# The mixers' residual gate, moved from the output weights to the output products

## Chip, core and metric

The kernel runs on one core of a Trainium2 chip. The metric is the device time of one execution in microseconds (us). Engines are named as the profile names them: PE is TensorE's matmuls, PEld its weight loads, DVE is VectorE, ACT is ScalarE, POOL is GpSimd, SP is SyncE, which issues most of the DMAs. L835 is line 835 of the kernel before.

## What is computed

Two layers of a streaming encoder over 256 tokens of width 1024, in float32. The place of the change is the first residual of each layer: a vector `1 + g_m`, one number for each of the 1024 columns, scales the output projection of three token mixers.

```python
def reference(x, c, positions, w_ada, ...):
    for l in range(DEPTH):                       # 2
        mod = (c_act @ w_ada[l] + b_ada[l])[:, None, :]
        sh_m, sc_m, g_m, sh_f, sc_f, g_f = jnp.split(mod, 6, axis=-1)
        h = x * (1.0 + sc_m) + sh_m
        mix = token_mixers(h, w_in[l], w_out[l], ...)     # [attention | retention | mLSTM] @ w_out
        x = layer_norm(DEEPNORM_ALPHA * x + (1.0 + g_m) * mix, ln_mix_g[l], ln_mix_b[l])
        h = x * (1.0 + sc_f) + sh_f
        y = moe_ffn(h.reshape(bsz * seq, d), w_router, b_router, w_gate[l], w_up[l], w_down[l])
        x = layer_norm(DEEPNORM_ALPHA * x + (1.0 + g_f) * y.reshape(bsz, seq, d), ...)
    return x
```

Since the gate scales columns, `(1 + g_m) * (o @ W)` is the same as `o @ (W * (1 + g_m))`.

## The kernel before

**Tiles.** Tokens lie on the 128 partitions in two tiles (tt = 0, 1), columns in halves of 512 (n = 0, 1). A product in float32 is split into a rounded part and a rest (`wsplit`: L415 casts the high part on ACT, L416 subtracts it on DVE), and three matmuls (L434 to L436) make one product of the two.

**Weights.** All weights come over one stream of DMAs on SP's queue, in an order written out by hand (`st.add` lines), into pools of buffers. A DMA is issued when its buffer is free, and everything behind it in the queue waits for it. The pool `ring` has 10 buffers of 512 KB, `w` 8, and `g0` one: it holds the mixers' gate `g1[l][0]`, and after it a down projection weight of the experts, ("dn", l, 1, 2).

**Order.** Each engine works through its instructions in a fixed order. A scheduler sets it when the program is built, with a simulated time line and priorities (`tc.high_priority`, `tc.issue_after`). So an edit at one place can change the order at others.

**The stage of the output projection**, once in each layer:

1. Retention and attention still finish: scores of retention on PE (L716), masked on DVE (L791, L792), sums over them on PE (L739), a norm on ACT and DVE with a matmul between (L760, L811, L812), attention's sums (L827), and the split of the mixers' output (L768, L769). Small instructions of the adaptive norm stand in between on DVE (L406, L411, L841 to L843, L935).
2. `out_w` fetches a tile of w_out (two blocks of 128 x 512); POOL multiplies each block in place with the gate (L917), with a high priority. `wsplit` splits it. Then PE multiplies (`out_part`): 16 blocks, each for two token tiles, three matmuls each. The four sums (tt, n) stay in four banks of PSUM; the last blocks close tile 0's two halves first, then tile 1's.
3. PE goes on with half of the sums of the adaptive norm (`ada_half`, L349, L353).
4. For each token tile, DVE forms the residual of two halves from x and PSUM (`residual`, L835), takes statistics of it (`lstat`, L442, L444), ACT makes the inverse deviation (rs, L210), and DVE normalizes 1024 columns (L957). PE transposes (L850), ACT and DVE copy (L961), PE multiplies with the router's weights (L963). ACT and POOL split the normalized tile (L972, L973). After tile 1 the router chooses experts, and the experts' stage (the MoE) begins.

POOL's memset of the next residual's buffer (`xrow`, L1039) waits for the last reading of x in step 4, since both use the same buffer. In the experts' stage PE multiplies (L1208, L1256, L1281), and DVE adds gathered rows (L1162).

Of the kernel before, what the change touches and what calls it, by code (L numbers as in the profile page):

```python
# [16 lines left out]
OP = mybir.AluOpType  # L17
# [10 lines left out]
ALPHA = (2.0 * L) ** 0.25  # L28
# [7 lines left out]
AHEAD_SPLIT = 400  # L36
# [78 lines left out]
def _trunk(ctx, tc, x_tok, x_chn, par, pos, rows, b_ada, w_ada, w_idx, w_in, w_out, w_gu, w_dn, out):  # L115
    nc = tc.nc
    V, A, G, PE = nc.vector, nc.scalar, nc.gpsimd, nc.tensor
# [17 lines left out]
    st = Stream(tc, sb, AHEAD)  # L135
# [10 lines left out]
    for l in range(L):  # L146
# [24 lines left out]
        st.add(("gu2", l, 1), w_gu[l, 1], 4, "S", range(2))  # L171
        st.add(("gu", l, 1), w_gu[l, 1], 8, which=(4, 5, 6, 7))
        st.add(("dn", l, 1), w_dn[l, 1], 4, "P", (0, 1))
        st.add(("dn", l, 1), w_dn[l, 1], 4, "g0", (2,))
        st.add(("gu4", l, 0), w_gu[l, 0], 16, "w", range(12, 16))
        st.add(("dn4", l, 1), w_dn[l, 1], 8, "w", (6, 7))
        st.add(("gu4", l, 2), w_gu[l, 2], 16, "w", (14, 15))
        st.add(("gu2", l, 2), w_gu[l, 2], 4, "O", (0,))
        st.add(("gu", l, 2), w_gu[l, 2], 8, which=range(2, 7))
# [649 lines left out]
            out_split(2 * g, 2, po)  # L829
        return oT  # L830

    def residual(z, x, p, tt, n):

        o = slice(tt * D + n * 512, tt * D + n * 512 + 512)
        V.scalar_tensor_tensor(z[:, o], x[:, o], ALPHA, p[tt][n], op0=OP.mult, op1=OP.add)  # L835
        return z[:, o]

    def make_aff(gcol, bcol, sc, sh, name):
# [15 lines left out]
    for l in range(L):  # L854
# [55 lines left out]
        def out_w(n, j):  # L910

            if j % 2 == 0:
                out_w.w = st.get(("out", l, n, j // 2))
                for i in range(2):
                    q = out_w.w[:, i * 512:(i + 1) * 512]
                    with tc.high_priority(offset=AHEAD_SPLIT):
                        G.tensor_tensor(q, q, g1[l][0][:, n * 512:(n + 1) * 512], op=OP.mult)  # L917
            return wsplit(out_w.w[:, (j % 2) * 512:(j % 2) * 512 + 512])

        for ns, js in (((0,), (0, 1, 2, 3)), ((1,), (0, 1, 2, 3)), ((0, 1), (4, 5))):  # L920
# [31 lines left out]
            for (la, na), q in zip(LAST[l], pa):  # L952
                ada_half(q, la, na, 0, True)
        for tt in range(2):
            m, rs = lstat([residual(z, xres, pd, tt, n) for n in range(2)])
            o = slice(tt * D, (tt + 1) * D)
            V.tensor_scalar(xn[:, o], z[:, o], m[:, 0:1], rs, op0=OP.subtract, op1=OP.mult)  # L957
            for k0 in (0, 4):
                pt = transposed(xn, tt, k0)
                q = h2[:, tt * D + k0 * P:tt * D + (k0 + 4) * P]  # L960
                (A.copy if k0 == 0 else V.tensor_copy)(q, pt)  # L961
                for k in range(k0, k0 + 4):
                    last = PE.matmul(pl[:, tt * E:(tt + 1) * E], h2v[:, tt, k, :], wrg[:, k, :], start=False, stop=(tt == 1 and k == KD - 1))  # L963
# [408 lines left out]
```

## Time and profile before

| | |
|---|---|
| runs | 730.05 us median of 3 (729.27 to 730.53) |
| profiled execution | 729.74 us |
| its span in the profile | 728.0 us |
| PE busy | 667.6 us (92%), mean granted clock 0.957 |
| DVE busy | 414.1 us (57%) |
| ACT busy | 280.9 us (39%) |
| POOL busy | 208.2 us (29%) |
| DMA | 204.19 MB, mean 280 GB/s |

The page's shares are means over stages with different limits. What one stage costs is read from its time line: which engine works without a pause, and what ends the pauses of the others. The granted clock is 1.00 where TensorE runs at 2.4 GHz and 0.50 where it runs at 1.2 GHz.

### The profile page before, as it was taken

The page shows a single profiled execution, that of the slowest core. Times are in us where ns is not written, and L with a number is a line of the kernel's source. Part 1 is how long each engine was busy: PE and PEld are TensorE (multiplying, and loading weights), DVE is VectorE, ACT ScalarE, POOL GpSimd, SP SyncE. Part 2 cuts the span into 40 slices and gives each one's busy share as a digit, 9 for nine tenths or more (in the row PEclk, how much of TensorE's full clock was granted, in tenths as well). Part 3 has the DMA queues.
Part 4 walks back from the last instruction along what each step waited for, and adds up shares of the span by engine and source line. Part 5 has one row for each costly group of instructions (what it writes and reads, how often), then busy time and mean ns, then how long its engine had stood idle before and what let it go on. Part 6 is the DMA issues. An engine that isn't in the chain of part 4 may idle for free. (4 is left out here: it accounts for less than half of the span.)

```text
span 728.0 us, 10437 instructions
## 1 busy us (share of the span) xinstructions
PE 667.6 (92%) x3638; PEld 409.9 (56%) x3638; DVE 414.1 (57%) x903; ACT 280.9 (39%) x583; POOL 208.2 (29%) x195
## 2 busy tenths in 40 slices
PE   5999699999898999999888999999899799999994
PEld 0567587864675434434347678885568554433431
DVE  5478986653975321243477999754645632234245
ACT  3346758344332212122256646944523212222131
POOL 3002933101913046102035613310740303712001
PEclk9999989999897999999998999999969789999998
DMA  8997773499986899999945773439958578999951
GB/s 305 407 368 241 258 267 112 144 363 409 377 299 236 310 322 349 370 408 407 365 156 172 235 256 116 144 125 319 396 183 276 187 264 304 354 353 407 406 193 58
DMA packets 57760, 204.19 MB, mean 280 GB/s; under 512 B 7336, under 2 KB 7464, under 8 KB 56422
## 3 DMA queue, kind: packets, MB, share of 16 engines
q1 hardware_dynamic: 55152, 198.49, 75.5%
q0 software_dynamic: 2112, 4.44, 1.6%
q8 instruction: 30, 0.49, 0.3%
q10 hardware_dynamic: 438, 0.54, 0.2%
q14 instruction: 28, 0.23, 0.1%
HBM read 202.15 MB, written 4.19 MB: 283 GB/s over the span
## 5 line engine op out<-in xcount | busy, mean ns | idle before, releaser
L416 DVE TENSOR_TENSOR sb_w<-sb_ring,sb_w 128x512 fp32r<-128x512 f32 (+1 forms) x156 | 117.1, 764 | 42.6 <-ACT sb_w L415 40.6
L415 ACT CAST sb_w<-sb_ring 128x512 fp32r<-128x512 f32 (+1 forms) x156 | 92.1, 608 | 89.0 <-PE ps_mm L435 44.2
L1208 PE MATMUL ps_s<-sb_ring,sb_S 128*64 128x512 f32 x424 | 116.2, 600 | 0.2 <-PEq L1117 0.2
L435 PE MATMUL ps_mm<-sb_w,sb_H 128*128 128x512 f32 (+2 forms) x224 | 79.9, 359 | 4.3 <-DVE sb_H L888 4.3
L434 PE MATMUL ps_mm<-sb_w,sb_H 128*128 128x512 f32 (+2 forms) x224 | 80.2, 365 | 1.9 <-ACT sb_w L415 1.3
L436 PE MATMUL ps_mm<-sb_w,sb_H 128*128 128x512 f32 (+2 forms) x224 | 74.9, 369 | 0.7 <-DVE sb_w L416 0.6
L917 POOL TENSOR_TENSOR sb_ring<-sb_ring,sb_g 128x512 f32<-128x512 f32 x32 | 45.5, 1460 | 72.0 <-DMA sb_ring<-w_out 70.8
L1208 PEld LDWEIGHTS ps_s<-sb_ring,sb_S 128*64 128x64 f32 x424 | 32.5, 136 | 54.0 <-issue 45.9
L349 PE MATMUL ps_t<-sb_ring,cact 128*32 128x512 f32 x272 | 47.7, 616 | 7.8 <-DVE posf L296 6.2
L434 PEld LDWEIGHTS ps_mm<-sb_w,sb_H 128*128 128x128 f32 x224 | 43.0, 194 | 10.7 <-ACT sb_w L415 2.8
L435 PEld LDWEIGHTS ps_mm<-sb_w,sb_H 128*128 128x128 f32 x224 | 43.3, 194 | 10.1 <-DVE sb_H L888 5.0
L436 PEld LDWEIGHTS ps_mm<-sb_w,sb_H 128*128 128x128 f32 x224 | 41.7, 194 | 11.6 <-issue 3.8
L1107 DVE TENSOR_SCALAR sb_S<-ps_t,afffg,afffb 128x256 f32<-128x256 f32 x32 | 17.4, 543 | 48.9 <-ACT sb_S L210 48.4
L1099 PEld LDWEIGHTS ps_t<-sb_O,sb_H 128*128 128x128 f32 x256 | 33.1, 193 | 19.9 <-issue 11.4
L1256 PE MATMUL ps_t<-sb_P,sb_sg 128*64 128x512 f32 x152 | 42.4, 599 | 0.5 <-ACT sb_sg L1243 0.5
L528 POOL TENSOR_TENSOR sb_rope<-sb_rope 128x256 f32<-128x256 f32 (+1 forms) x16 | 15.8, 990 | 89.3 <-DVE iwm L564 31.5
L435 PE MATMUL ps_mm<-sb_H,sb_w 128*128 128x256 f32 x128 | 37.3, 292 | 3.9 <-DVE sb_w L416 3.9
L1099 PE MATMUL ps_t<-sb_O,sb_H 128*128 128x256 f32 x256 | 39.0, 297 | 2.0 <-DVE sb_O L1029 1.8
L633 POOL TENSOR_SCALAR sb_sg<-sb_sg,sm 128x128 f32<-128x128 f32 (+1 forms) x32 | 26.6, 847 | 45.5 <-DVE sm L630 23.3
L210 ACT ACTIVATE sb_S<-ps_t,afffb,afffg 128x256 f32<-128x256 f32 x32 | 18.0, 563 | 55.9 <-PE ps_t L1099 55.1
L434 PE MATMUL ps_mm<-sb_H,sb_w 128*128 128x256 f32 x128 | 37.1, 291 | 0.0
L436 PE MATMUL ps_mm<-sb_H,sb_w 128*128 128x256 f32 x128 | 36.9, 288 | 0.0
(369 smaller groups left out, 1234.1 us busy)
## 6 DMA issues: line engine op xcount, KB each, us to landing
sb_ring<-w_gu SPq DMA_DIRECT2D x106, 512.0 KB, 7.4
sb_ring<-w_ada SPq DMA_DIRECT2D x96, 512.0 KB, 6.9
sb_P<-w_dn SPq DMA_DIRECT2D x58, 512.0 KB, 7.9
sb_ring<-w_in SPq DMA_DIRECT2D x56, 512.0 KB, 6.1
sb_ring<-w_out SPq DMA_DIRECT2D x16, 512.0 KB, 10.1
sb_S<-w_gu SPq DMA_DIRECT2D x6, 1024.0 KB, 8.4
sb_row<-rows SPq DMA_DIRECT2D x8, 512.0 KB, 9.6
sb_w<-w_gu SPq DMA_DIRECT2D x12, 256.0 KB, 4.7
```

Of the source, the lines that this page charges most:

```text
L210: return A.activation(o, i, f, bias=bias, scale=scale)
L349: PE.matmul(pa[32 * g:32 * g + 32, :], cact[:, k:k + 1].to_broadcast([P, 32]), w[g // 2][:, (g % 2) * 512:(g % 2) * 512 + 512], start=(i = ...
L415: A.copy(hi, src)
L416: V.tensor_tensor(lo, src, hi.bitcast(F32), op=OP.subtract)
L434: PE.matmul(o, a[0], b[0], start=start, stop=False)
L435: PE.matmul(o, a[1], b[0], start=False, stop=False)
L436: return PE.matmul(o, a[0], b[1], start=False, stop=stop)
L633: G.tensor_scalar(sg[:, i * n:(i + 1) * n], sg[:, i * n:(i + 1) * n], sm[:, h:h + 1], None, op0=OP.mult)
L917: G.tensor_tensor(q, q, g1[l][0][:, n * 512:(n + 1) * 512], op=OP.mult)
L1099: last = PE.matmul(pt[:, j * 256:(j + 1) * 256], src[:, tt * D + k * P:tt * D + (k + 1) * P], oh[:, tt * D + q * 256:tt * D + (q + 1) * 25 ...
L1208: PE.matmul(pgu[s * 64:s * 64 + 64, :], xg[:, c0:c0 + 64], ws[s][k], start=(i == order[0] and k == 0), stop=(i == order[3] and k == 1), ti ...
L1256: PE.matmul(pyb[s * 64:s * 64 + 64, :], hdT[:, k, s * 64:s * 64 + 64], wd[s][k], start=(k == 0), stop=(k == 1), tile_position=(0, 64 * s))
```

## The change

The gate no longer multiplies the weights. `out_w` loses the two POOL products for each tile of w_out. `residual` gets the gate and becomes two DVE instructions: the product of PSUM with the gate into z, then `ALPHA * x + z` in place. The gate is now read until the residual, so its buffer comes free later, and the weight that takes it over, ("dn", l, 1, 2), stands two entries later in the stream.

```diff
         st.add(("dn", l, 1), w_dn[l, 1], 4, "P", (0, 1))
-        st.add(("dn", l, 1), w_dn[l, 1], 4, "g0", (2,))
         st.add(("gu4", l, 0), w_gu[l, 0], 16, "w", range(12, 16))
         st.add(("dn4", l, 1), w_dn[l, 1], 8, "w", (6, 7))
+        st.add(("dn", l, 1), w_dn[l, 1], 4, "g0", (2,))
...
-    def residual(z, x, p, tt, n):
+    def residual(z, x, p, g, tt, n):
 
         o = slice(tt * D + n * 512, tt * D + n * 512 + 512)
-        V.scalar_tensor_tensor(z[:, o], x[:, o], ALPHA, p[tt][n], op0=OP.mult, op1=OP.add)
+        V.tensor_tensor(z[:, o], p[tt][n], g[:, n * 512:(n + 1) * 512], op=OP.mult)
+        V.scalar_tensor_tensor(z[:, o], x[:, o], ALPHA, z[:, o], op0=OP.mult, op1=OP.add)
         return z[:, o]
...
                 out_w.w = st.get(("out", l, n, j // 2))
-                for i in range(2):
-                    q = out_w.w[:, i * 512:(i + 1) * 512]
-                    with tc.high_priority(offset=AHEAD_SPLIT):
-                        G.tensor_tensor(q, q, g1[l][0][:, n * 512:(n + 1) * 512], op=OP.mult)
...
-            m, rs = lstat([residual(z, xres, pd, tt, n) for n in range(2)])
+            m, rs = lstat([residual(z, xres, pd, g1[l][0], tt, n) for n in range(2)])
```

The scheduler then orders the engines anew. Three places, all in layer 0; lines of the changed kernel are one higher from the residual on (its product is L835, its second instruction L836), and three lower behind `out_w` (L957 is L954 there, L961 is L958, L963 is L960).

DVE at the residual, before (sb_H is z, bs and mv are the statistics):

```order
L835 SCALAR_TENSOR_TENSOR sb_H<-sb_X,ps_mm 128x512
L442 BN_STATS bs<-sb_H 128x6
L835 SCALAR_TENSOR_TENSOR sb_H<-sb_X,ps_mm 128x512
L442 BN_STATS bs<-sb_H 128x6
L835 SCALAR_TENSOR_TENSOR sb_H<-sb_X,ps_mm 128x512
L444 BN_AGGR mv<-bs 128x2
L442 BN_STATS bs<-sb_H 128x6
L835 SCALAR_TENSOR_TENSOR sb_H<-sb_X,ps_mm 128x512
L957 TENSOR_SCALAR sb_H<-sb_H,mv,rs 128x1024
L442 BN_STATS bs<-sb_H 128x6
L444 BN_AGGR mv<-bs 128x2
L957 TENSOR_SCALAR sb_H<-sb_H,mv,rs 128x1024
```

The same place after, behind the first product (sb_g_631 is the gate):

```order
L836 SCALAR_TENSOR_TENSOR sb_H<-sb_X,sb_H 128x512
L835 TENSOR_TENSOR sb_H<-ps_mm,sb_g_631 128x512
L442 BN_STATS bs<-sb_H 128x6
L836 SCALAR_TENSOR_TENSOR sb_H<-sb_X,sb_H 128x512
L835 TENSOR_TENSOR sb_H<-ps_mm,sb_g_631 128x512
L442 BN_STATS bs<-sb_H 128x6
L835 TENSOR_TENSOR sb_H<-ps_mm,sb_g_631 128x512
L836 SCALAR_TENSOR_TENSOR sb_H<-sb_X,sb_H 128x512
L444 BN_AGGR mv<-bs 128x2
L836 SCALAR_TENSOR_TENSOR sb_H<-sb_X,sb_H 128x512
L442 BN_STATS bs<-sb_H 128x6 x2
L954 TENSOR_SCALAR sb_H<-sb_H,mv,rs 128x1024
```

All four products stand ahead of the first normalization, and so does the last statistic, which came behind it before; layer 1 has the same order.

ACT at the end of retention, before (sb_e<-ps_s is the square of L739's sums):

```order
L820 COPY sb_S<-ps_mm 128x512 x2
L415 CAST sb_w<-sb_ring 128x512
L210 ACTIVATE sb_e<-ps_s 128x512
L415 CAST sb_w<-sb_ring 128x512 x2
L210 ACTIVATE sb_e<-ps_s,epsc 128x512
```

The same place after:

```order
L820 COPY sb_S<-ps_mm 128x512 x2
L415 CAST sb_w<-sb_ring 128x512 x3
L210 ACTIVATE sb_e<-ps_s 128x512
L415 CAST sb_w<-sb_ring 128x512 x3
L210 ACTIVATE sb_e<-ps_s,epsc 128x512
```

Two more blocks of w_out are cast ahead of the square, for which ACT waits on PE.

PE at the router, before (L850 transposes, L963 is the router's product):

```order
L850 MATMUL ps_t<-ident,sb_H 128x128 x8
L963 MATMUL ps_s<-wrg,sb_O 128x16 x4
L850 MATMUL ps_t<-ident,sb_H 128x128 x4
L963 MATMUL ps_s<-wrg,sb_O 128x16 x4
L850 MATMUL ps_t<-ident,sb_H 128x128 x4
L963 MATMUL ps_s<-wrg,sb_O 128x16 x8
```

The same place after:

```order
L851 MATMUL ps_t<-ident,sb_H 128x128 x8
L960 MATMUL ps_s<-wrg,sb_O 128x16 x8
L851 MATMUL ps_t<-ident,sb_H 128x128 x8
L960 MATMUL ps_s<-wrg,sb_O 128x16 x8
L349 MATMUL ps_mm<-sb_ring,cact 32x512 x8
```

Four of tile 0's router products move from behind tile 1's first transposes to ahead of them, which is the order that layer 1 had already.

## Rows read from the trace of the kernel before

**Rows 1.** The page's part 5: busy, mean of one, idle ahead, and its releaser.

```profile
L917 POOL TENSOR_TENSOR sb_ring<-sb_ring,sb_g 128x512 f32<-128x512 f32 x32 | 45.5, 1460 | 72.0 <-DMA sb_ring<-w_out 70.8
```

**Rows 2.** Time line of POOL in layer 0: start, length, instruction, idle ahead.

```profile
179.47 24.30 POOL L917 TENSOR_TENSOR sb_ring<-sb_ring,sb_g 128x512 f32<-128x512 f32 x16 [39.13 <-DMA sb_ring<-w_out]
218.45 1.80 POOL L1039 MEMSET sb_X<- 128x2048 f32 x1 [14.68 <-DVE sb_H L835]
221.96 2.34 POOL L973 TENSOR_TENSOR sb_H<-sb_H 128x1024 fp32r<-128x1024 f32 x1 [1.71 <-ACT sb_H L972]
```

**Rows 3.** Time line of PE in layer 0.

```profile
181.87 1.45 PE L716 MATMUL ps_s<-sb_S 64*128 64x256 f32 x8 [1.24 <-DVE sb_S L792]
185.46 2.83 PE L739 MATMUL ps_s<-sb_S 128*64 128x128 f32 x24 [2.15 <-DVE sb_S L792]
...
225.88 1.72 PE L963 MATMUL ps_s<-wrg,sb_O 128*128 128x16 f32 x8
```

**Rows 4.** Time line of DVE in layer 0, end of retention.

```profile
177.36 0.16 DVE L411 TENSOR_TENSOR modc<-mod,bada 128x4 f32<-128x4 f32 x1
...
179.47 1.81 DVE L769 TENSOR_TENSOR sb_O<-sb_e,sb_O 128x512 fp32r<-128x512 f32 x1 [0.68 <-ACT sb_O L768]
...
182.46 1.19 DVE L411 TENSOR_TENSOR modc<-mod,bada 128x4 f32<-128x4 f32 x1
183.69 1.19 DVE L841 TENSOR_TENSOR affmg<-pr,modc 128x8 f32<-128x8 f32 x1
...
185.33 0.77 DVE L842 TENSOR_TENSOR affmb<-pr,modc 128x8 f32<-128x8 f32 x1
...
186.36 0.28 DVE L792 TENSOR_TENSOR sb_S<-ps_s,dec 128x128 f32<-128x128 f32 x1
```

**Rows 5.** Time line of DVE in layer 0, residual and normalization.

```profile
213.60 0.69 DVE L835 SCALAR_TENSOR_TENSOR sb_H<-sb_X,ps_mm 128x512 f32<-128x512 f32 x1 [0.67 <-PE ps_mm L436]
...
217.70 0.69 DVE L835 SCALAR_TENSOR_TENSOR sb_H<-sb_X,ps_mm 128x512 f32<-128x512 f32 x1
218.30 2.50 DVE L957 TENSOR_SCALAR sb_H<-sb_H,mv,rs 128x1024 f32<-128x1024 f32 x1
...
222.34 2.51 DVE L957 TENSOR_SCALAR sb_H<-sb_H,mv,rs 128x1024 f32<-128x1024 f32 x1 [0.70 <-ACT rs L210]
```

**Rows 6.** Time line of DVE in layer 1, end of retention.

```profile
522.12 1.31 DVE L416 TENSOR_TENSOR sb_w<-sb_ring,sb_w 128x512 fp32r<-128x512 f32 x1 [1.59 <-ACT sb_w L415]
...
523.55 1.02 DVE L411 TENSOR_TENSOR modc<-mod,bada 128x4 f32<-128x4 f32 x1
...
525.80 0.68 DVE L772 TENSOR_TENSOR sb_e<-ps_s,sb_e 128x512 f32<-128x512 f32 x1
...
547.19 0.68 DVE L769 TENSOR_TENSOR sb_O<-sb_e,sb_O 128x512 fp32r<-128x512 f32 x1
```

**Rows 7.** Time line of PE in layer 1.

```profile
526.53 1.65 PE L716 MATMUL ps_s<-sb_S 64*128 64x256 f32 x4 [2.88 <-DVE sb_e L772]
...
568.91 1.09 PE L850 MATMUL ps_t<-ident,sb_H 128*128 128x128 f32 x8 [1.36 <-DVE sb_H L957]
...
573.06 1.94 PE L850 MATMUL ps_t<-ident,sb_H 128*128 128x128 f32 x8 [0.63 <-DVE sb_H L957]
```

**Rows 8.** Stretches: length, busy of PE, PEld, DVE, ACT, POOL, clock, DMA, GB/s.

```profile
183.80:190.60 6.80, 5.14 (x29) 4.25 (x30) 6.38 (x9) 1.62 (x3) 6.80 (x6) 0.50 1.04 417
190.60:217.60 27.00, 27.00 (x160) 21.42 (x158) 22.72 (x27) 10.94 (x20) 13.17 (x8) 1.00 0.91 315
...
525.40:538.60 13.20, 11.36 (x32) 7.98 (x34) 7.45 (x16) 1.85 (x3) 10.71 (x9) 0.50 0.52 193
```

**Rows 9.** The same view of a stretch of layer 0's experts.

```profile
310.00:330.00 20.00, 19.44 (x81) 7.95 (x78) 8.96 (x16) 4.62 (x9) 1.81 (x1) 1.00 1.03 409
```

**Rows 10.** Waits of PE, and of PEld, from 236 to 364: total, times, longest.

```profile
PE ps_t L1241 <- DVE sb_rope L1239: 1.8, 1, 1.8
...
PEld ps_s L1208 <- DMA sb_P<-w_dn: 0.3, 1, 0.3
```

## The prediction

> **What bounds the kernel now.** I read the page first: TensorE is busy most of the time, so what counts is where PE pauses, and where it runs at the lower of its two clocks. Then I read the time lines of POOL, PE and DVE side by side in the two stages that the change touches, the end of retention with the output projection and the residual with the router, and last the waits of PE in the experts' stage.
>
> In layer 0 POOL multiplies weights without a break from 179.47 to 203.77 [rows 2]; both layers together cost it 45.5 us [rows 1]. POOL itself is waited for by few. But DVE instructions that read two inputs from SBUF are slow in just that time. L411 on 4 columns takes 0.16 us with POOL idle and 1.19 with POOL at work; L769 takes 1.81, and 0.68 in layer 1 after POOL's last product [rows 4, 6]. Those slow instructions stand ahead of L791 and L792 in DVE's order, and PE waits on L792 twice, for 1.24 and 2.15 us [rows 3]. After that PE has no pause to the end of the output projection [rows 8]. So in this stage the path to the end runs through DVE up to about 186.6 (the last L792 ends there [rows 4]), and through PE from there. Layer 1 has the same picture: L416 takes 1.31, L411 1.02, and PE waits 2.88 us on L772 [rows 6, 7]. In both places TensorE's granted clock then is 0.50, that is 1.2 GHz, for 6.8 and 13.2 us, with 5.14 and 11.36 us of PE work in it [rows 8].
>
> In the tail the path runs through DVE again: residual, statistics, normalization L957, and PE's transposes wait for L957 (1.36 and 0.63 us in layer 1 [rows 7]). L957 itself takes 2.5 us, and why is seen from POOL: the memset runs from 218.45 to 220.25 and L957 ends at 220.80; L973 runs from 221.96 to 224.30 and the second L957 ends at 224.85 [rows 2, 5]. Both times L957 ends 0.55 us after POOL.
>
> **The change part by part.** The sum is made against the profiled execution, 729.74 us (a span of 728.0 and 1.74 around it). The median of the runs is 0.31 above that.
>
> *The holes, layer 0.* Without POOL's products, L769 falls from 1.81 to 0.69 and L411 from 1.19 to 0.16, and L841, as small as L411, from 1.19 to the same 0.16 [rows 4, 6]. That is 1.12 + 1.03 + 1.03 = 3.2 us ahead of the L792 that starts L739. L842 gives 0.6 more (0.77 to 0.16) ahead of the last L792, which lets L739 finish: 3.8. Behind it PE is dense, so this moves the whole rest of the stage. I take 3.5, between the two ends. The new order has nothing that gives it back: ACT casts two blocks more ahead of the square, but ACT waited there anyway, and the DMA of the blocks was ahead of POOL, whose products ran without a pause [rows 2].
>
> *The holes, layer 1.* L416 falls from 1.31 to 0.69 and L411 from 1.02 to 0.16. From L411's end at 524.57 to L772 at 525.80 there are 1.23 us with L841 and L842 [rows 6]. In the new order L935 and L843 go ahead of L772 as well: three small ones at 0.16 and one of 128 columns at about 0.28 (L792's time [rows 4]) are 0.76. So 0.62 + 0.86 + 0.47 = 1.9 us. The ends are 1.5 (what the gaps between instructions may keep) and 3.0 (if PE's four L716, 1.65 us at the lower clock [rows 7], still run at the higher one). I take 1.9.
>
> *The clock.* If TensorE keeps 2.4 GHz through the shorter holes, half of its work there is saved: 5.14 / 2 = 2.6 us in layer 0, 11.36 / 2 = 5.7 in layer 1 [rows 8]; if it falls as before, nothing. In layer 0 the 3.4 us of pauses shrink to a few tenths, so I take 2.0 of the 2.6. In layer 1 nearly a microsecond of waiting on L772 is left, and thin work around it, so I take nothing. Ends: 0 and 8.3.
>
> *The tail's DVE.* Four products are added in each layer. From the first L835 at 213.60 to the last at 217.70 six instructions (and L444) pass, 0.68 us each [rows 5]. In the new order nine stand ahead of the last L836, since all four products come first: 3 x 0.68 = 2.05 us later. A product from PSUM is priced as L835 was, 0.69, since that read PSUM and SBUF too; the second instruction, now all from SBUF, as L769 with POOL idle, 0.68. POOL's memset follows the last reading of x, and L957 ends 0.55 behind the memset, so L957 moves by 2.05 and no more: the two statistics that now stand ahead of it run beside the memset. ACT's cast and POOL's L973 follow L957, and the second L957 follows L973: 2.05 again.
>
> What PE makes of it differs. In layer 1 PE waits for both L957 already, so all of it is paid: 2.05 at least, 3.0 if the clock falls sooner and the first eight transposes take 1.94 instead of 1.09 [rows 7]. I take 2.1. In layer 0 router products of tile 0, 1.72 us [rows 3], stood behind tile 1's transposes. They now fill the longer wait: between 2.05 - 1.72 = 0.3 and 2.05. I take 1.2. In all DVE gets 8 x 0.69 = 5.5 us more, of which 3.3 is on the path.
>
> The Trainium skill, SBUF — State Buffer, section on the two separate sides, says that DVE and GpSimd take turns on one pair of ports, with an exclusive lock: the one that comes second waits for the whole instruction of the other. The two endings 0.55 behind POOL agree [rows 2, 5]. If the pair were shared by bandwidth instead, L957 would keep its 2.5 us and start 2.05 + 2 x 0.68 later, 3.4 in each layer, and the sum below would be 2.7 us worse. The rule also speaks against the change: L836 reads two inputs from SBUF, which L835 did not, and so could be blocked; but POOL idles for 14.68 us up to the memset [rows 2].
>
> *The queue.* The DMA into the gate's buffer now waits for the last product, and behind it stand only weights of later experts. Cost nothing; the tiles around it wait for PE's last blocks anyway. If that cover were gone, it would hold the queue for 2 us, the tail's delay.
>
> *The experts' order.* The scheduler moves some L1162, L1208 and L1281. PE's longest pause there is 1.8 us, on a DVE instruction [rows 10]; I take 0, with 1.8 either way.
>
> Sum: -3.5 - 1.9 - 2.0 + 1.2 + 2.1 + 0 = -4.1. The profiled execution goes to 725.6, the median to 726.0, with a range of its own from 722.0 to 729.0.
>
> **Rivals.**
>
> *The clock stays high in both holes.* Then 8.3 instead of 2.0 is saved: 719.7. For it: the holes lose most of their idle time. Against: in layer 1 a fall followed a single wait of 2.88 us, and PE's work around it stays thin.
>
> *The gain is hidden by the DMA.* In layer 0's experts the DMA engines are full at 409 GB/s for 20 us [rows 9]. If weights set the end there, an earlier start and a later one both vanish, and the time stays at 730.05. Against: the longest wait of PE's loads for a weight is 0.3 us [rows 10].
>
> *The tail loses its clock, and the kernel gets slower.* If the longer wait for the first L957 makes the clock fall at once, then in each layer the first eight transposes take 0.85 more [rows 7] and tile 0's sixteen router products 1.7 more (two times 1.72 [rows 3], against half of it). A tail then costs 2.05 + 0.85 + 1.7 = 4.6, two 9.2, against 5.4 from the holes with no gain of clock: 733.9. It decides from where the two tails cost more than 5.4. Against: in layer 1 the eight transposes ran at the higher clock right after 1.36 us of waiting [rows 7].
>
> That POOL is not relieved can't be: its products are gone from the order.
>
> **How the numbers follow.** Forecast 0.62, clock high in both holes 0.13, hidden 0.13, slower 0.12. The range from 719.7 to 731.0 reaches from the first rival to past the second and leaves out the third and a little more. About 0.2% (1.5 us) is what a measurement of this kernel can tell from no change. Faster than that: 0.58 of the forecast and 0.13, 0.71. Within it: 0.04 and 0.13, 0.17. Slower: 0.12.
>
> **What would show it.** Right, if in the profile after, L769, L411 and L841 at the end of retention take 0.69 and 0.16, PE's waits on L792 shrink to a few tenths, and L1's wait on L772 to about one microsecond; if the first L957 ends about 2.4 us behind the last L836, and the stretch from the end of the output projection to the router's choice is 1 to 2 us longer in each layer. Wrong, if these DVE instructions stay slow, if the granted clock falls in the tail before tile 0's transposes, or if PE waits for weights in the experts' stage.

## The result and the profile after

The changed kernel takes 719.74 us (median of 4 runs, 718.52 to 721.6), the kernel before, measured beside it, 729.66 (4 runs). The ratio is 0.9877, 95% interval 0.9847 to 0.9908: about 9 us less. The forecast was 726.0, with a range of its own from 722.0 to 729.0 and a whole range from 719.7 to 731.0. The sign was right, and the gain is more than twice the forecast. The time lies outside the forecast's own range. It lies inside the whole range by 0.04 us, and only because that range was drawn to the time of the first rival, whose clock stays high in both holes (719.7, with a chance of 0.13). So that the range holds is luck, and the rival is what came. The profiled execution of after takes 720.78 us, its span is 719.0 (728.0 before).

The lines that the prediction named, in the profile after (lines are one higher behind the residual, and three lower behind `out_w`). POOL in layer 0, time line (start, length, instruction, idle ahead), which answers to [rows 2]; the products are gone:

```profile
215.05 1.80 POOL L1036 MEMSET sb_X<- 128x2048 f32 x1 [73.67 <-DVE sb_H L836]
218.56 2.35 POOL L970 TENSOR_TENSOR sb_H<-sb_H 128x1024 fp32r<-128x1024 f32 x1 [1.71 <-ACT sb_H L969]
```

DVE at the end of retention in layer 0, which answers to [rows 4], and PE beside it, to [rows 3]:

```profile
180.51 0.69 DVE L769 TENSOR_TENSOR sb_O<-sb_e,sb_O 128x512 fp32r<-128x512 f32 x1 [0.69 <-ACT sb_O L768]
...
182.38 0.17 DVE L411 TENSOR_TENSOR modc<-mod,bada 128x4 f32<-128x4 f32 x1
182.58 0.17 DVE L842 TENSOR_TENSOR affmg<-pr,modc 128x8 f32<-128x8 f32 x1
```

```profile
181.80 1.44 PE L716 MATMUL ps_s<-sb_S 64*128 64x256 f32 x8
183.43 1.53 PE L739 MATMUL ps_s<-sb_S 128*64 128x128 f32 x24 [0.19 <-DVE sb_S L792]
```

L769 takes 0.69 in place of 1.81 us, and the two small ones 0.17 in place of 1.19. PE's two waits of 1.24 and 2.15 us have become none and 0.19, and L739 runs in 1.53 us and not in 2.83, since the clock no longer falls.

Layer 1, DVE (answers to [rows 6]) and PE (to [rows 7]):

```profile
519.63 0.16 DVE L411 TENSOR_TENSOR modc<-mod,bada 128x4 f32<-128x4 f32 x1
519.83 0.17 DVE L842 TENSOR_TENSOR afffg<-pr,modc 128x8 f32<-128x8 f32 x1
...
520.36 0.69 DVE L772 TENSOR_TENSOR sb_e<-ps_s,sb_e 128x512 f32<-128x512 f32 x1
```

```profile
521.11 1.45 PE L716 MATMUL ps_s<-sb_S 64*128 64x256 f32 x8 [0.47 <-DVE sb_e L772]
...
558.76 1.09 PE L851 MATMUL ps_t<-ident,sb_H 128*128 128x128 f32 x8 [2.89 <-DVE sb_H L954]
```

PE's wait on L772 is 0.47 us (2.88 before). In the tail PE waits 2.89 us for the first normalization (1.36 before).

The tail on DVE in layer 0, which answers to [rows 5]:

```profile
208.66 0.69 DVE L835 TENSOR_TENSOR sb_H<-ps_mm,sb_g 128x512 f32<-128x512 f32 x1 [1.61 <-PE ps_mm L436]
...
214.35 0.64 DVE L836 SCALAR_TENSOR_TENSOR sb_H<-sb_X,sb_H 128x512 f32<-128x512 f32 x1
...
216.10 1.30 DVE L954 TENSOR_SCALAR sb_H<-sb_H,mv,rs 128x1024 f32<-128x1024 f32 x1
...
219.29 2.17 DVE L954 TENSOR_SCALAR sb_H<-sb_H,mv,rs 128x1024 f32<-128x1024 f32 x1
```

Both L954 end 0.55 us behind POOL's work (217.40 behind 216.85, 221.46 behind 220.91), as both L957 did before. Stretches with the granted clock (columns as in [rows 8]):

```profile
181.80:212.60 30.80, 30.61 (x194) 25.06 (x194) 19.98 (x39) 13.24 (x23) 0.00 (x0) 1.00 0.99 392
...
219.70:233.10 13.40, 13.40 (x56) 8.96 (x56) 6.29 (x31) 3.00 (x5) 3.57 (x2) 0.50 0.59 219
519.70:540.00 20.30, 19.03 (x141) 14.99 (x142) 10.39 (x25) 8.81 (x15) 0.00 (x0) 1.00 0.93 324
561.00:578.00 17.00, 14.54 (x63) 10.69 (x64) 10.28 (x50) 3.55 (x6) 3.58 (x2) 0.50 0.37 133
310.00:330.00 20.00, 18.07 (x84) 8.94 (x80) 9.57 (x17) 5.57 (x11) 3.79 (x3) 1.00 1.03 409
```

No stretch of either hole is at 0.50 any more, where [rows 8] had 6.8 and 13.2 us of it. In the tails the clock falls as before, behind tile 0's transposes, but for longer. The kernel before has these stretches at the lower clock:

```profile
224.80:234.90 10.10, 9.90 (x48) 7.28 (x48) 3.93 (x24) 2.41 (x4) 2.35 (x1) 0.50 0.50 184
573.00:586.50 13.50, 10.97 (x47) 7.75 (x47) 8.07 (x47) 2.93 (x5) 2.35 (x1) 0.50 0.36 120
```

The experts' stage moves as much data as in [rows 9].

### Where the time went

One table serves the rest. For each layer it gives two stretches of the profiled execution, from starts of instructions: from the first scores of retention (first L716) to the end of the output projection (first L349 behind it), and from there to the first gather of the experts (first L1099, L1096 after). The time is the median of all runs, for e5 of five of its six (719.6 to 723.6), since one was disturbed. Each ratio is to the kernel before as measured beside that kernel; its median was 727.7 us beside e1 to e3 and 729.6 to 729.8 beside the others. One execution stands behind each row's stretches, so tenths count in the first stretch, which repeats within 0.05 us where nothing falls, and about 1 us in the second.

| kernel | L0: to the end of the projection | L0: to the first gather | L1: to the end | L1: to the gather | time, ratio to before [interval] |
|---|---|---|---|---|---|
| before | 38.7 | 19.7 | 42.9 | 17.4 | 729.7 |
| after | 32.7 | 21.7 | 34.2 | 19.7 | 719.7, 0.9877 [0.985, 0.991] |
| after, again | 32.7 | 20.6 | 34.2 | 20.0 | 718.0, 0.9840 [0.982, 0.987] |
| e1, POOL's products to a spare | 39.9 | 20.6 | 40.3 | 20.0 | 733.4, 1.0081 [1.005, 1.011] |
| e2, no products at all | 32.7 | 18.3 | 34.2 | 18.2 | 719.3, 0.9887 [0.986, 0.991] |
| e3, layer 0 alone | 32.7 | 21.7 | 42.2 | 17.4 | 724.5, 0.9949 [0.993, 0.997] |
| e3, layer 1 alone | 37.6 | 18.3 | 34.2 | 20.0 | 724.6, 0.9956 [0.994, 0.998] |
| e4, two idle products | 32.7 | 20.1 | 36.6 | 20.3 | 722.2, 0.9902 [0.987, 0.993] |
| e4, four idle products | 32.7 | 20.6 | 37.9 | 20.4 | 725.4, 0.9945 [0.992, 0.997] |
| e8, before with PE kept busy | 37.7 | 19.8 | 37.5 | 17.4 | 724.8, 0.9925 [0.991, 0.995] |
| e5, POOL late | 32.7 | 17.3 | 34.2 | 18.9 | 722.1, 0.9897 [0.987, 0.992] |
| e6, tile order | 32.7 | 18.8 | 34.2 | 18.2 | 717.0, 0.9815 [0.979, 0.984] |
| e7, both | 32.7 | 18.7 | 34.2 | 17.4 | 717.0, 0.9829 [0.981, 0.985] |
| e7, again | 32.7 | 18.6 | 34.2 | 17.3 | 717.0, 0.9820 [0.980, 0.984] |

Before to after, by the two profiled spans (-9.0): the first scores start 1.0 later, ahead of the change; the holes and the clock give -6.0 in layer 0 and -8.7 in layer 1; the tails take +2.0 and +2.3; from layer 0's first gather to layer 1's scores nothing changes (285.5 and 285.4); layer 1's experts to the end +0.3. The 1.0 at the start is no effect of the change: the first scores start between 176.2 and 179.9 in the profiles of all these kernels.

### The profile page after: what moved, and what is told of

Same layout as the page of the kernel before. It is cut to its first block, busy times and chain, and to the rows that moved or that the text cites. A ratio compares the mean times of both kernels' runs of the same rounds, so it can differ in the third digit from the quotient of the medians.

```text
span 719.0 us, 10379 instructions
## 1 busy us (share of the span) xinstructions
PE 665.7 (93%) x3638; PEld 410.1 (57%) x3638; DVE 399.6 (56%) x911; ACT 281.2 (39%) x583; POOL 161.4 (22%) x163
## 5 line engine op out<-in xcount | busy, mean ns | idle before, releaser
L416 DVE TENSOR_TENSOR sb_w<-sb_ring,sb_w 128x512 fp32r<-128x512 f32 (+1 forms) x156 | 109.8, 715 | 44.7 <-ACT sb_w L415 43.1
L1205 PE MATMUL ps_s<-sb_ring,sb_S 128*64 128x512 f32 x424 | 113.8, 601 | 0.2 <-PEq L1114 0.2
L349 PE MATMUL ps_t<-sb_ring,cact 128*32 128x512 f32 x272 | 48.0, 621 | 7.2 <-DVE posf L296 6.2
L434 PEld LDWEIGHTS ps_mm<-sb_w,sb_H 128*128 128x128 f32 x224 | 43.7, 197 | 11.3 <-ACT sb_w L415 2.7
L435 PEld LDWEIGHTS ps_mm<-sb_w,sb_H 128*128 128x128 f32 x224 | 44.0, 197 | 9.1 <-DVE sb_H L889 4.0
L436 PEld LDWEIGHTS ps_mm<-sb_w,sb_H 128*128 128x128 f32 x224 | 42.3, 197 | 12.1 <-issue 3.8
L1104 DVE TENSOR_SCALAR sb_S<-ps_t,afffg,afffb 128x256 f32<-128x256 f32 x32 | 17.4, 543 | 51.7 <-ACT sb_S L210 51.7
L1096 PEld LDWEIGHTS ps_t<-sb_O,sb_H 128*128 128x128 f32 x256 | 33.1, 193 | 19.9 <-issue 12.2
L1096 PE MATMUL ps_t<-sb_O,sb_H 128*128 128x256 f32 x256 | 38.9, 297 | 2.0 <-DVE sb_O L1026 1.8
L435 PE MATMUL ps_mm<-sb_H,sb_w 128*128 128x256 f32 x128 | 38.1, 298 | 2.8 <-DVE sb_w L416 2.8
L434 PE MATMUL ps_mm<-sb_H,sb_w 128*128 128x256 f32 x128 | 37.9, 298 | 0.0
L436 PE MATMUL ps_mm<-sb_H,sb_w 128*128 128x256 f32 x128 | 37.9, 296 | 0.0
L1036 POOL MEMSET sb_X<- 128x2048 f32 x2 | 3.6, 1804 | 151.3 <-DVE sb_H L836 151.3
## 6 DMA issues: line engine op xcount, KB each, us to landing
sb_ring<-w_out SPq DMA_DIRECT2D x16, 512.0 KB, 10.1
```

Source lines behind the costliest of these rows:

```text
L349: PE.matmul(pa[32 * g:32 * g + 32, :], cact[:, k:k + 1].to_broadcast([P, 32]), w[g // 2][:, (g % 2) * 512:(g % 2) * 512 + 512], start=(i = ...
L416: V.tensor_tensor(lo, src, hi.bitcast(F32), op=OP.subtract)
L434: PE.matmul(o, a[0], b[0], start=start, stop=False)
L435: PE.matmul(o, a[1], b[0], start=False, stop=False)
L436: return PE.matmul(o, a[0], b[1], start=False, stop=stop)
L1096: last = PE.matmul(pt[:, j * 256:(j + 1) * 256], src[:, tt * D + k * P:tt * D + (k + 1) * P], oh[:, tt * D + q * 256:tt * D + (q + 1) * 25 ...
```

## Experiments

**POOL's products on a spare tile (e1).** Is it POOL's work beside DVE, or that the weights waited for POOL? The kernel after, with

```diff
+        spare = wk.tile([P, 512], F32, name="spare", tag="spare")
...
                 out_w.w = st.get(("out", l, n, j // 2))
+                for i in range(2):
+                    q = out_w.w[:, i * 512:(i + 1) * 512]
+                    with tc.high_priority(offset=AHEAD_SPLIT):
+                        G.tensor_tensor(spare, q, g1[l][0][:, n * 512:(n + 1) * 512], op=OP.mult)
```

> The kernel after, with POOL's 32 products put back where they stood (same inputs, same count, same place in POOL's order), but written to a spare tile that nobody reads. So the weights no longer wait for POOL, DVE keeps the gate's products, and only POOL's work beside DVE is back. Theory (POOL's products slow DVE's small instructions, PE waits for these, and the clock falls in the wait): DVE's L411 and L842 at the end of retention take about 1.1 us again, PE's first L716 and L739 wait 1 to 3 us, the granted clock falls to 0.50 in both places, and nearly all of the 14.6 us that the two stages gained is lost, while the tails' extra cost stays: 730 to 735 us, at or above the kernel before. Rival (the gain came from the weights that need not wait for POOL, or from the new order): it stays within 1.5 us of 719.7.

Measured: 733.4 us, above the kernel before. Layer 1's hole is back, in the order of the kernel after. DVE in layer 1, and the stretch behind PE's wait, which is 2.79 us on L772:

```profile
523.23 0.44 DVE L411 TENSOR_TENSOR modc<-mod,bada 128x4 f32<-128x4 f32 x1
523.70 0.17 DVE L842 TENSOR_TENSOR afffg<-pr,modc 128x8 f32<-128x8 f32 x1
523.79 1.24 DVE L843 TENSOR_TENSOR afffb<-pr,modc 128x8 f32<-128x8 f32 x1
...
525.15 1.22 DVE L844 TENSOR_TENSOR afffb<-afffb,modc 128x8 f32<-128x8 f32 x1
526.29 0.68 DVE L772 TENSOR_TENSOR sb_e<-ps_s,sb_e 128x512 f32<-128x512 f32 x1
```

```profile
525.60:535.50 9.90, 8.47 (x23) 6.30 (x24) 6.41 (x12) 1.24 (x2) 9.35 (x8) 0.50 0.69 257
```

Which small instruction is caught depends on where POOL stands: here L843 and L844, before L411 and L841. In layer 0 the picture is a different one with the same cost. The expected 1.1 us came for L842 (1.14) but not for L411 (0.16), and PE waits less at the scores: 1.06 us on L792, with the clock at 0.50 for 3.3 us behind it. Later, DVE's subtractions of the weights (L416) and L769 are slow, and PE waits on one L416 for 1.6 us and on L769 for 1.5. DVE's groups from 176 to 216 in e1, and from 178 to 213 in after (busy, mean in ns):

```profile
L416 DVE TENSOR_TENSOR sb_w<-sb_ring,sb_w 128x512 fp32r<-128x512 f32 x16 | 19.1, 1224 | 3.7 <-ACT sb_w L415 3.7
```

```profile
L416 DVE TENSOR_TENSOR sb_w<-sb_ring,sb_w 128x512 fp32r<-128x512 f32 x16 | 10.8, 688 | 6.8 <-ACT sb_w L415 5.7 <-DMA sb_ring<-w_ada 1.1
```

So POOL's work itself is the cost, 7.1 us in layer 0 and 6.1 in layer 1 by the table, with nobody waiting for its results. The rival on the weights falls, and so does the new order, which e1 keeps. POOL still reads each weight, so its buffer comes free later; but in this stage of layer 0 ACT's casts of the weights wait for PE and DVE alone (11.5 us in sum), never for a transfer. DVE's instructions that read PSUM keep their times beside POOL: in the kernel before L406 takes 0.16 us there, L772 0.68, L791 0.41 and L792 0.28, as in the kernel after within 0.01.

**One layer alone (e3).** Of the kernel after, one layer goes back to POOL's products, to the old residual and to the old place in the stream. For layer 0 alone (layer 1 alone has `l != 1` and `l == 1`):

```diff
+                for i in range(2 if l != 0 else 0):
+                    q = out_w.w[:, i * 512:(i + 1) * 512]
+                    with tc.high_priority(offset=AHEAD_SPLIT):
+                        G.tensor_tensor(q, q, g1[l][0][:, n * 512:(n + 1) * 512], op=OP.mult)
...
-            m, rs = lstat([residual(z, xres, pd, g1[l][0], tt, n) for n in range(2)])
+            m, rs = lstat([residual(z, xres, pd, g1[l][0] if l == 0 else None, tt, n) for n in range(2)])
```

> The change in layer 0 alone; layer 1 keeps POOL's products and the old place of its last down-projection tile in the stream. Theory (each layer's hole pays by itself: layer 0 gains 6.0 to the end of the projection, gives back 2 in the tail and 1 to the lower clock behind it, and gains 1 in the experts' stage): 725 to 727 us. Rival (the layers hang together: with 3 to 4 us less in layer 0, layer 1's hole changes as well): under 723 us.

> The change in layer 1 alone. Theory (layer 1 gains 8.7 us to the end of the projection, of which about 6 are the clock that no longer falls, and gives back 2.3 in the tail): 723 to 724.5 us, with the granted clock at 1.00 through the stretch that had 0.50 for 13.2 us. Rival (the clock stayed high in layer 1 only because of what changed before it): the clock falls there as before, and the time is 727 us or more.

Measured: 3.7 us less than before with layer 0 alone (interval 2.0 to 5.4), 3.2 with layer 1 alone (1.8 to 4.6). The times expected are missed by 0.5 and 0.1 us, but the kernel before was 727.7 beside these runs, 2 us under what they started from, so layer 1's share is smaller than expected. Neither rival holds: the first stretch is short in the layer that has the change, and in that one alone. Where layer 1 lacks it, the clock falls there once more, in another execution:

```profile
522.20:532.30 10.10, 9.28 (x22) 6.58 (x23) 5.74 (x12) 1.10 (x2) 9.47 (x8) 0.50 0.49 178
```

Layer 1's stretches in the profile gain 8.0 to 8.7 and give back 2.3 to 2.6, so that 5 to 6 us should be left, and the runs show 3.2. The profiled run of that kernel is the fastest of nine (720.3, the others 723.0 to 726.8); of the others there is no trace, and what they lose is open. Together the two layers make 6.9 us, less than the 9.0 of the whole change and the 11.7 of its second measurement (e0, below), so that the two simply add up is not shown.

**PE kept busy in the hole of the kernel before (e8).** This prices the clock by itself. The kernel before, POOL's products and all, gets 32 matmuls of 128x128 that nobody reads, between the first group of scores and the one that waits for L772 in layer 1:

```diff
+        def idle(spare, n, behind):
+            for _ in range(n):
+                with tc.issue_after(behind.ins):
+                    behind = PE.matmul(spare, hT[0][:, 0:128], hT[0][:, 0:128], start=True, stop=True)
+            return behind
...
+                    if fill and k0 and 2 * j + s < 2:
+                        m = idle(pq[s][:, 384:512], (32, 0)[s], m)
```

> The kernel before, POOL's products and all, with 32 idle matmuls of 128x128 on PE in layer 1's hole (into the unused quarter of the scores' bank), between the first L716 group and the one that waits 2.88 us for L772. DVE and POOL do what they did. Theory (about 6 us of layer 1's gain are TensorE's clock, which falls because PE has nothing to do): with PE busy the clock stays at 1.00, the stretch from the first scores to the end of the output projection takes 37 to 39 us and not 42.9, and the time is 723.5 to 726. Rival (the clock falls because of the kind of work around the hole, scores of 64 rows and transposes, or by chance): 0.50 for 9 to 13 us as in the kernel before, 729 to 731 us, or more if the idle matmuls outlast the wait.

Measured: 724.8 us, ratio 0.9925: 5.5 us less than before (4.0 to 6.9) for work that does nothing. PE in the hole (L713 is the idle matmul, L724 the scores), DVE beside it (L851 and L853 are L841 and L843 of before), and the stretches:

```profile
523.40 0.92 PE L724 MATMUL ps_s<-sb_S 64*128 64x256 f32 x4 [0.34 <-ACT sb_e L210]
524.25 3.79 PE L713 MATMUL ps_s<-sb_H 128*128 128x128 f32 x32
527.97 0.92 PE L724 MATMUL ps_s<-sb_S 64*128 64x256 f32 x4
```

```profile
523.60 1.03 DVE L411 TENSOR_TENSOR modc<-mod,bada 128x4 f32<-128x4 f32 x1
524.66 1.20 DVE L851 TENSOR_TENSOR afffg<-pr,modc 128x8 f32<-128x8 f32 x1
...
527.16 1.24 DVE L853 TENSOR_TENSOR afffb<-afffb,modc 128x8 f32<-128x8 f32 x1
```

```profile
523.40:531.60 8.20, 8.20 (x52) 7.16 (x52) 7.24 (x14) 2.82 (x5) 8.20 (x7) 1.00 0.87 319
523.40:561.00 37.60, 36.10 (x238) 29.49 (x242) 24.62 (x41) 13.71 (x24) 15.98 (x11) 1.00 0.81 288
```

DVE's instructions are as slow as before, POOL works through the whole hole, and PE starts the next scores 1.4 us later than L772 would have let it (its end, 526.5). Yet the clock stays at 1.00, and the stretch to the end of the projection falls from 42.9 to 37.5. So in layer 1 the larger part was never the wait, it was the clock behind it. The edit also changes the order of the scores in this layer, and the later ones moved behind the first blocks of the projection, which can be worth up to the 0.7 us that PE waited there before.

**A wait made by hand (e4).** The reverse: the kernel after, with two or four idle products on DVE ahead of L772 in layer 1 and no POOL work:

```diff
         rstd = head_rstd(pcn)
-        V.tensor_tensor(rstd, pcn, rstd, op=OP.mult)
+        with tc.high_priority(offset=AHEAD_SPLIT) if l else nullcontext():
+            if l:
+                spare = wk.tile([P, 512], F32, name="spare", tag="spare")
+                for _ in range(2):
+                    V.tensor_tensor(spare, pcn, rstd, op=OP.mult)
+            V.tensor_tensor(rstd, pcn, rstd, op=OP.mult)
```

> The kernel after with two idle products on DVE (PSUM times rstd into a spare tile, 0.6 us each in a row) ahead of L772 in layer 1, so that PE's second group of L716 waits about 2.2 us for L772 instead of 0.47. Theory (what layer 1 lost before was its wait and then the clock behind the wait): if 2.2 us of waiting make the granted clock fall, the stretch from the first L716 to the end of the output projection grows from 34.2 to 39 to 41 us, and the time is 724 to 726; if not, by the two products alone, to 35 to 36 us, and the time is 720.5 to 722. Rival (the clock fell for another reason than the wait on DVE, POOL's work at the same time among them): the clock stays at 1.00 here and with twice the wait.

> The same with four idle products in place of two: a wait of 3 to 4 us, as long as the 2.88 of the kernel before or longer, and with no POOL work in it. Theory: the granted clock falls to 0.50 behind the wait, and the stretch from the first L716 to the end of the projection takes 40 to 43 us, as in the kernel before (42.9); 725 to 728 us. Rival (without POOL's work the clock stays): 36 to 37.5 us for the stretch, and 722 to 723.5 us.

Measured: 722.2 and 725.4 us. The wait is not the single long one that was meant, since the scheduler put the masks of the scores (L796, L797 here) between the idle products. PE with two of them (L777 is L772 of after):

```profile
520.27 0.92 PE L716 MATMUL ps_s<-sb_S 64*128 64x256 f32 x4 [1.00 <-DVE sb_S L797]
521.60 2.01 PE L716 MATMUL ps_s<-sb_S 64*128 64x256 f32 x8 [0.41 <-DVE sb_e L777]
```

with four:

```profile
519.39 2.97 PE L716 MATMUL ps_s<-sb_S 64*128 64x256 f32 x8 [0.94 <-DVE sb_S L797]
```

and the stretches at the lower clock, with two and with four:

```profile
522.30:525.60 3.30, 3.30 (x11) 2.51 (x11) 1.77 (x5) 0.00 (x0) 0.00 (x0) 0.51 0.97 347
```

```profile
518.30:525.10 6.80, 5.87 (x26) 4.37 (x24) 4.17 (x10) 0.62 (x1) 0.00 (x0) 0.50 0.82 298
```

The clock falls with POOL idle, so the rival that ties it to POOL's work is out. But the stretch grows by 2.4 and 3.7 us, not by the 5 to 9 of the forecast: two waits of 1.00 and 0.41 bring 3.3 us at half clock, two of 1.00 and 0.94 bring 6.8, the 2.88 and 0.71 of before 13.2, but the 2.98 and 0.82 of e3 10.1. So a longer wait is not simply a longer fall, and what sets the length is not shown. In the kernel after PE waits 0.47 in this place; the 0.34 ahead of the first scores are in all these kernels. The time with two lies between the two forecasts. With four it is in the forecast range (725.4), but the profile is of the fastest of the seven runs (721.7 to 728.0), so the others may have fallen for longer than the 6.8 us that it shows.

**After, again (e0).** Was it chance that the clock stayed? The same kernel once more, measured beside e6, e7 and e8.

> The kernel after once more, unchanged, as the measure for the others of this call. Theory: 718.5 to 721.6 us as before, ratio to the kernel before 0.985 to 0.991, with the granted clock at 1.00 through layer 1's hole. Rival (the clock kept high there by chance in the one execution that was profiled): a second profile shows 0.50 for some microseconds behind L772.

Measured: 718.0 us, half a microsecond under the range expected, ratio 0.9840. In the second profile nothing falls in this place either:

```profile
516.00:536.00 20.00, 18.72 (x140) 14.74 (x141) 10.37 (x24) 8.58 (x15) 0.00 (x0) 1.00 0.93 333
```

**No products at all (e2).** What do the tails pay for DVE's products? This kernel leaves the mixers' gate out:

```diff
-        V.tensor_tensor(z[:, o], p[tt][n], g[:, n * 512:(n + 1) * 512], op=OP.mult)
-        V.scalar_tensor_tensor(z[:, o], x[:, o], ALPHA, z[:, o], op0=OP.mult, op1=OP.add)
+        V.scalar_tensor_tensor(z[:, o], x[:, o], ALPHA, p[tt][n], op0=OP.mult, op1=OP.add)
```

> The kernel after without its eight products on VectorE (the residual is one instruction again, as in the kernel before; the mixers' gate is left out of the result). Theory (each layer's tail is 2.0 to 2.3 us longer because of the products, which stand on the path between the projection and the router): 714.5 to 717.5 us, and the stretch from the last matmul of the output projection to the first gather as long as in the kernel before. Rival (the products lie beside other work, and the tails are longer for the lower clock alone): within 1 us of 719.7.

Measured: the tails are shorter, 18.3 and 18.2 against 20.6 to 21.7 and 19.7 to 20.0 (the kernel before has 19.7 and 17.4). Yet the time is 719.3, ratio 0.9887: no gain over after. The expectation failed in what follows the tail. From layer 0's first gather to layer 1's first scores it is 289.5 us, where before, after and after again have 284.8 to 285.5. So the 2.3 to 3.4 us of a shorter tail in layer 0 bought nothing, since 4 us came back behind it. Part of that is the clock, which falls once more among layer 0's experts:

```profile
317.30:320.60 3.30, 3.30 (x9) 1.41 (x8) 0.00 (x0) 0.00 (x0) 2.49 (x3) 0.50 1.04 413
```

All kernels have one fall behind layer 0's experts (it starts between 372 and 382 us). Those whose profile shows a further one before layer 1's scores (e1, e2, e4, e5, e7, e8) take 286.1 to 290.7 us from layer 0's first gather to these scores, the six without it 284.8 to 285.5. Of 3.3 us at half clock 1.7 are lost; what else e2 loses is open.

**The tail's order (e5, e6, e7).** e5 makes POOL's memset and its subtraction wait until tile 1 is normalized, through a one-column memset on DVE into their outputs:

```diff
-            V.tensor_scalar(xn[:, o], z[:, o], m[:, 0:1], rs, op0=OP.subtract, op1=OP.mult)
+            normal = V.tensor_scalar(xn[:, o], z[:, o], m[:, 0:1], rs, op0=OP.subtract, op1=OP.mult)
...
+        xrow = sb("X")
+        with tc.issue_after(normal.ins):
+            for q in (xrow, xl):
+                V.memset(q[:, 0:1].bitcast(F32), 0.0)
+        G.memset(xrow, 0.0)
...
-        xrow = sb("X")
-        G.memset(xrow, 0.0)
```

e6 instead puts tile 1's products behind tile 0's statistics on DVE, and e7 does both:

```diff
-            m, rs = lstat([residual(z, xres, pd, g1[l][0], tt, n) for n in range(2)])
+            with tc.issue_after(lstat.last.ins) if tt else nullcontext():
+                parts = [residual(z, xres, pd, g1[l][0], tt, n) for n in range(2)]
+            m, rs = lstat(parts)
```

> The kernel after with POOL's two works of the tail (the memset of the experts' rows and the low parts of tile 0) made to wait until tile 1's normalization is done, by a one-column memset on DVE that each of them must follow. Theory (the normalization L954 cannot run beside POOL's work: in the kernel after it ends 0.55 us behind POOL's memset in tile 0 and 0.55 us behind POOL's subtraction in tile 1): both L954 take about 0.65 to 1.3 us without the 0.6 and 0.9 to 1.5 us of waiting, each tail is 1 to 2 us shorter, and the time is 716 to 718.5. Rival (other work ends each tail, the clock and PE's matmuls of the router): within 1 us of 719.7.

> The same, and DVE's order in the tail changed as well: tile 1's products come behind tile 0's mean and variance, so that tile 0's normalization and transposes start about 1.5 to 2.5 us earlier, and the chain of tile 1 is not longer (DVE has the same instructions and loses the idle 0.4 to 1 us in which it waits for ACT's rstd). Theory (in the tail DVE's order sets the time): each tail 2 to 4 us shorter than after, end of the projection to the first gather 16 to 18 us, and 713 to 717 us. Rival (tile 1's chain, which starts later, is what ends the tail): no better than the run with POOL's work moved alone.

> The kernel after with DVE's new order in the tail alone (tile 1's products behind tile 0's statistics); POOL's memset and subtraction stay where they are. Theory (both parts count, since L954 cannot run beside POOL's work): between the kernel after and the one with both, 718 to 719 us, tails 0.5 to 1.5 us shorter than after's in layer 1, and tile 1's L954 still ending about 0.55 us behind POOL. Rival (the order alone brings the gain): as good as both, within 0.7 us.

> Both parts again (POOL's work late and DVE's order), beside the kernel after in the same call. Theory (layer 1's tail is 2.3 us shorter; of what layer 0's tail gains, the experts' stage behind it swallows most, since the weights' transfers end it): 2 to 4 us less than the kernel after. Rival (the gain of the earlier call was chance): within 1 us of it.

Measured: with POOL out of the way both normalizations take 0.8 us. DVE in e5, layer 0:

```profile
213.46 0.80 DVE L954 TENSOR_SCALAR sb_H<-sb_H,mv,rs 128x1024 f32<-128x1024 f32 x1
...
214.98 0.81 DVE L954 TENSOR_SCALAR sb_H<-sb_H,mv,rs 128x1024 f32<-128x1024 f32 x1 [0.60 <-ACT rs L210]
```

In e6 the first stands ahead of POOL's memset (0.81) and the second beside POOL's subtraction, and it ends 0.56 behind it (218.81 behind 218.25):

```profile
216.85 1.96 DVE L956 TENSOR_SCALAR sb_H<-sb_H,mv,rs 128x1024 f32<-128x1024 f32 x1 [0.60 <-ACT rs L210]
```

```profile
215.91 2.34 POOL L972 TENSOR_TENSOR sb_H<-sb_H 128x1024 fp32r<-128x1024 f32 x1
```

So the waiting is shown, and taking it away shortens layer 0's tail by 3 to 4 us. The time of e5 is no better than after's (0.9897), for the reason of e2: 290.7 us from the first gather to layer 1's scores, 5 more than after. ACT's first copy of the experts' hidden rows in layer 0 (L1240, L1243 in e5) comes 7.0 us earlier than in after (251.19 for 258.18; 2.6 of it because the first scores start earlier), the last one 1.0 earlier (359.87 for 360.83). In e5 that stage runs with a lower mean clock, beside DMA at 384 GB/s:

```profile
310.00:330.00 20.00, 17.65 (x75) 8.38 (x72) 6.42 (x11) 4.50 (x9) 3.79 (x3) 0.91 0.99 384
```

The clock explains about 1.8 us of it (9% of 20). The scheduler also gave the experts another order, and PE shows no long wait for a weight; the rest stays open. e6, with a tail 2 to 3 us shorter than after's in layer 0 and 1.5 to 1.9 in layer 1, keeps what it gains (285.0 in that stretch). It and e7 are the fastest kernels, 717.0 us each. Beside them after took 718.0, so the order is worth about 1 us there, less than these intervals can tell. POOL's late start adds nothing to it in time: layer 1's tail is 0.8 us shorter in e7 than in e6, but e7 has the further fall of the clock among the experts (286.8 and 287.1 us for 285.0). Of the four expectations, e5's is missed (722.1 for 716 to 718.5), e6 comes as its rival has it, as good as both, e7's 717.0 is at the edge of its range with a longer tail than expected in layer 0 (18.7), and e7 again is within 1 us of after, as its rival has it.

## Why the prediction was right, and where it was not

**Layer 0's hole and clock.** Predicted -3.5 and -2.0, measured -6.0 together. The instructions named fell to the values named, and the clock stayed at 1.00. Right, by the reason given: e1 shows POOL's work as the cause, though in layer 0 it comes in part through other DVE instructions (L416, L769). The Trainium skill, SBUF — State Buffer, section on the two separate sides, tells of an exclusive lock between DVE and GpSimd on one pair of ports. e1 (L843 and L844, of 8 columns, at 1.24 and 1.22 us beside POOL) and e5 (L954 at 0.80 us without POOL, 1.30 and 2.17 beside it) agree with it.

**Layer 1's hole.** Predicted -1.9 (1.5 to 3.0). From the first scores to PE's next group it is 3.79 us before and 1.38 after, -2.4. Of the half microsecond over the forecast 0.3 lies in L406, which no longer stands behind a slow L416 at all, and 0.2 in the five small instructions ahead of L772, which start 0.08 to 0.21 us apart though each lasts 0.16 to 0.29.

**Layer 1's clock: the step that failed.** The prediction took nothing of 5.7 us, because "nearly a microsecond of waiting on L772 is left, and thin work around it". The wait left is 0.47 us, and the clock does not fall. From PE's second group of scores to the end of the projection it takes 39.12 us before and 32.86 after: -6.3, of which 0.7 is a second wait on L792 and the rest the clock. e8 finds it by the other way, with 5.4 us less in the stretch although the idle matmuls outlast the wait by 1.4. The term's size was right in the rival (5.7; the 6.3 without the second wait are 5.6), but the sum put it at nothing, and the rival had a chance of 0.13. e4 shows how near the decision was: with waits of 1.00 and 0.41 the clock falls, if only for 3.3 us. The half microsecond by which the hole was misjudged lies just there.

**The tails.** Predicted +1.2 and +2.1, measured +2.0 and +2.3 in the first profile, +0.9 and +2.6 in the second. The sums are near, but in part by luck: the two terms in them were off in opposite directions. The first normalization ends 2.41 us behind the last L836, as worked out (2.4). But it moved by 1.5 us and not by 2.05: from the first L349 behind the projection to its end it is 3.21 us before (220.80) and 4.74 after (217.40), since the nine instructions ahead of the last L836 take 5.69 us, 0.63 each and not 0.68. The rest is the clock, which the sum put at nothing here. In layer 1 tile 0's router products (L963, L960 after) now run at the lower clock. PE in layer 0 before and after, then in layer 1 before and after:

```profile
217.59 1.06 PE L349 MATMUL ps_mm<-sb_ring,cact 128*32 128x512 f32 x8
```

```profile
212.66 1.06 PE L349 MATMUL ps_mm<-sb_ring,cact 128*32 128x512 f32 x8
```

```profile
570.47 1.96 PE L963 MATMUL ps_s<-wrg,sb_O 128*128 128x16 f32 x16 [0.47 <-ACT sb_O L961]
```

```profile
560.51 3.31 PE L960 MATMUL ps_s<-wrg,sb_O 128*128 128x16 f32 x16 [0.65 <-ACT sb_O L958]
```

In layer 1 of the second profile the eight transposes take 1.97 us too, so there the clock did fall ahead of them. That is the mechanism of the third rival; in layer 1 it cost 0.8 us in the first profile and 1.1 in the second, not the 2.55 of the rival, because the longer products fill waits that PE had there, 0.63 us on the second L957 among them.

**The experts' order, the queue, DMA.** Predicted 0, measured 0 from layer 0's first gather to layer 1's scores. The second rival (a gain hidden in the experts' stage) did not act on this change: layer 0's first gather comes 3.0 us earlier than before in the first profile, 6.0 in the second and 7.8 in e6, and nothing of it is lost behind. Its effect is seen in e2 and e5, which come 9.6 and 10.0 us earlier than before and lose 4 and 5; the cause is shown only for the part of the clock.

So the sum was 4.9 us short, of which the clock of layer 1 with the second wait is 6.3, the two holes 1.0, and in the other direction the tails 1.0 and the later start and end 1.4.

## What to carry to other kernels

Before an engine is given work because it has time to spare, look at which other engine's instructions it holds up: here 45 us of POOL's multiplications, waited for by few, cost 6 to 7 us in each layer (e1) through DVE instructions, of 0.16 us that became 1.2 and of 0.69 that became 1.2 to 1.8. Price a pause of PE together with the work right behind it, at both clocks, and as long as the pause that is left is uncertain by half a microsecond, keep both. A few idle matmuls in a pause are a cheap way to learn what the clock costs there, and may pay by themselves (e8: 5.5 us).

## What the runs showed of the hardware that was not expected

- POOL's memset, which reads nothing, holds up DVE's normalization: 1.30 us beside it, 0.80 without. The statistics L442 beside the same memset are not held up (two in 1.28 us). The Trainium skill, SBUF — State Buffer, section on the two separate sides, has the exception for a GpSimd op that does not read SBUF only for DVE ops with two SBUF inputs, and names DVE's faster two-port modes without it; the 0.80 us for 1024 columns, where a product of 512 takes 0.69, fit such a mode; that L957 and L954 ran in one is not shown.
- The time at the lower clock is not fixed: 3.3, 6.8, 9.9, 10.1 and 13.2 us in layer 1's hole, behind waits of 1.4 to 3.8 us in sum, and not in the order of the waits.
- The start of the first scores differs by 3.7 us (176.2 to 179.9) between profiles of kernels that are alike up to there. A single profile's span is no measure for 1 or 2 us.
